# Scaling attention after P·V instead of scaling P, with heads sharing score banks, in a two-layer decoder kernel

## The chip, the cores and the metric

The kernel runs on one core of one Trainium2 chip. The metric is the device time of one execution in microseconds (us). Before the change it is 1733.85 us, the median of 3 runs (1732.92 to 1735.76). Engines are named as in the profile: PE is TensorE, DVE is VectorE, ACT is ScalarE, POOL is GpSimd, SP is SyncE.

## The reference

A decoder of two layers: width 1024, 512 tokens, float32. Each layer normalises x, projects it once, and feeds four token mixers of 4 heads x 64 whose outputs are joined and projected; then come cross attention over 256 memory rows and a SwiGLU.

```python
for l in range(DEPTH):
    h = rms_norm(x, norm_mix[l])
    c_hg, c_dsa, c_nsa, c_ml = split_cols(h @ w_in[l], GROUP_COLS)
    mixed = concatenate([hgrn2_mixer(c_hg, ...), dsa_mixer(c_dsa, ...), nsa_mixer(c_nsa, ...), mlstm_mixer(c_ml, ...)])
    x = x + mixed @ w_out[l]
    x = x + cross_attention(rms_norm(x, norm_xa[l]), rms_norm(mem, norm_mem[l]), ...)
    x = x + swiglu(rms_norm(x, norm_ffn[l]), ffn_w13[l], ffn_w2[l])

def masked_softmax(s, mask):
    s = where(mask, s, -inf);  m = max(s, -1);  e = exp(s - m)
    return e / sum(e, -1)

# DSA:  softmax(q k^T / 8, over the keys that an indexer picked) v
# NSA:  gate0 * softmax(q k_cmp^T / 8) v_cmp + gate1 * softmax(q k_sel^T / 8) v_sel + gate2 * softmax(q k_win^T / 8) v_win
# cross attention:  softmax(q k_mem^T / 8) v_mem
```

A softmax here is exp of the scores less their maximum, divided by its row sum; NSA multiplies each of its three outputs by a gate of each head and token. The HGRN2 mixer and the mLSTM mixer are recurrences in chunks and have no softmax over keys.

## The kernel before

**Tiling.** 512 tokens are 4 blocks of 128 (`tb` 0 to 3). Projections run as three products of split operands (xh·wh, xl·wh, xh·wl; lines L294 to L296 and L304 to L306). DSA and NSA attend blockwise: block `tb` sees the first `n = (tb + 1) * 128` keys. NSA calls `attend` twice in each block (selected keys, then window keys), DSA once: 12 calls in a layer. Cross attention (`xa`) has a loop of its own over the 4 blocks.

**One head in `attend`.** PE makes 128 x n scores in a PSUM bank `sc` (L513, L514) and adds the mask (L516 or L519). DVE takes the row maximum (L467). ACT makes P = exp(s - max) with the row sum (L469). DVE takes the reciprocal (L521) and multiplies P by it, in NSA by the gate too (L523, L525). PE transposes P in blocks of 128 x 128 into the bank `tp` (L458), ACT copies that to SBUF as PT (L462). After two heads PE multiplies with the values into the bank `o` (L533). The result is transposed: 64 rows for each head, 128 tokens along the free axis.

**Around it.** In DSA, `o` is split from PSUM into `xh` (ACT, L671) and `xl` (DVE, L672, recorded at the helper's line L316) for the output projection. In NSA a third, compressed attention (`compressed`, L1095 on) puts its output into the same bank `o` first (L1109); the two calls of `attend` accumulate onto it, and ACT copies the sum to `mo[2]` (L1124). `xa` handles two heads at a time: scores L1271 and L1272, maximum L1273, exp L1280, reciprocal L1282, scaling of P L1283 (at L316), transposes L458, P·V L1290, then xh L1298 and xl L1299 (at L316).

**PSUM.** In the stage with NSA the banks are `tp` 1, `sc` 2, `o` 1, `dt` 1, `mb` 1 and `acc` 2. In the stage with DSA they are `tp` 1, `sc` 1, `o` 1, `dt` 1, `hb` 2; there DSA's transposes go to `dt`. In `xa`: `tp` 2, `sc` 2, `o` 2.

**What sets the order.** Mixers are generators: their `yield` values are costs, and a weaver alternates between generators by these. The tile framework's scheduler then fixes one order of instructions for each engine. A layer has these stages (times of layer 0, then layer 1): the projection for DSA (0 to 30, then from 891.5); A, NSA and mLSTM with DSA's choice of keys (30 to 300.5; 892 to 1150.2), in which NSA attends from 117 and from 975; B, DSA's attention with HGRN2 and the first part of the output projection (300.5 to 430; 1150.2 to 1277); cross attention (430 to 500; 1277 to 1347); SwiGLU (500 to 891.5; 1347 to 1723). A last part of stage A (from 241 and from 1099.3, the "tail" below) has only NSA's block 3 and the end of mLSTM. L424 makes, in another stage, a factor for each token the same on all partitions: four float32 matmuls of a column against a diagonal.

Of the kernel before, what the change touches and what calls it, by code (L numbers as in the profile page):

```python
# [7 lines left out]
FT = mybir.dt.float32  # L8
# [3 lines left out]
AF = mybir.ActivationFunctionType  # L12
# [190 lines left out]
class Kernel:  # L203
# [260 lines left out]
    def softmax_unit(self, pool, sc, n, nmax, den):  # L464

        nc = self.nc
        nc.vector.tensor_reduce(nmax, sc[:, :n], axis=AX.X, op=OP.max, negate=True)  # L467
        p = self.t(pool, "P", [128, S], bufs=2)
        nc.scalar.activation(p[:, :n], sc[:, :n], AF.Exp, bias=nmax, accum_out=den)  # L469
        return p  # L470

# [30 lines left out]
    def attend(self, pool, tb, q, kst, v, mask, which, o, first, last, gate=None):  # L502

        nc = self.nc
        stat = self.t(pool, "stat", [128, 3, 4])
        n = (tb + 1) * 128
        for hp in range(2):
            pT = []  # L510
            for h in (2 * hp, 2 * hp + 1):
                sc = self.psum("sc", pool=pool)
                nc.tensor.matmul(sc[:, :n], q[0][:, h], kst[:, :n], start=True, stop=False, skip_group_check=True)  # L513
                nc.tensor.matmul(sc[:, :n], q[1][:, h], kst[:, :n], start=False, stop=False, skip_group_check=True)  # L514
                if mask is None:
                    nc.tensor.matmul(sc[:, n - 128:n], self.identb, self.trib, start=False, stop=True,  # L516
                                     skip_group_check=True)
                else:
                    nc.tensor.matmul(sc[:, :n], self.identb, mask, start=False, stop=True, skip_group_check=True)  # L519
                p = self.softmax_unit(pool, sc, n, stat[:, 0, h:h + 1], stat[:, 1, h:h + 1])  # L520
                nc.vector.reciprocal(stat[:, 2, h:h + 1], stat[:, 1, h:h + 1])  # L521
                if gate is None:
                    nc.vector.tensor_scalar(p[:, :n], p[:, :n], stat[:, 2, h:h + 1], None, op0=OP.mult)  # L523
                else:
                    nc.vector.tensor_scalar(p[:, :n], p[:, :n], stat[:, 2, h:h + 1], gate[:, h:h + 1],  # L525
                                            op0=OP.mult, op1=OP.mult)
                pT.append(self.t(pool, "PT", [128, S], bufs=3))
                ev = self.act_copy
                self.transpose_blocks(pT[-1][:, :n], lambda j: p[:, j * 128:j * 128 + 128], tb + 1, ev, pool=pool)
                yield 0.4 + 0.2 * tb  # L530
            for sb in range(tb + 1):
                for e in range(2):
                    nc.tensor.matmul(o[64 * e:64 * e + 64, hp], v(sb), pT[e][:, sb * 128:sb * 128 + 128],  # L533
                                     start=(first and sb == 0), stop=(last and sb == tb), skip_group_check=True)
            yield 0.2 + 0.2 * tb
# [89 lines left out]
    def dsa_attn(self, pool):  # L625
# [35 lines left out]
        for tb in range(TB):  # L661
            qb = nxt
            yield 1.0
            if tb < TB - 1:
                nxt = prepare(tb + 1)
            yield 1.0
            o = self.psum("o", (128, 2, 128))
            yield from self.attend(pool, tb, qb, kst, lambda sb: kv[:, sb, 64:128], masks[tb], 0, o, True, True)
            for c in range(2):
                (xh, xl), b = self.d_out[c], slice(tb * 128, tb * 128 + 128)  # L670
                nc.scalar.activation(xh[:, b], o[:, c], AF.Copy)  # L671
                self.tt(xl[:, b], o[:, c], xh[:, b].bitcast(FT), OP.subtract)  # L672
# [318 lines left out]
    def nsa(self, pool):  # L991
# [103 lines left out]
        def compressed(tb, e, o):  # L1095
# [11 lines left out]
            self.transpose_blocks(eT, lambda j: e.rearrange("p a b -> p (a b)"), 1, self.act_copy)  # L1107
            for hp in range(2):
                nc.tensor.matmul(o[:, hp], vbd[:, 2 * hp:2 * hp + 2].rearrange("p a b -> p (a b)"), eT,  # L1109
                                 start=(hp == 0), stop=False, skip_group_check=True)  # L1110

        nxt = prepare(0)
        for tb in range(TB):
            e, qb = nxt
            o = self.psum("o", (128, 2, 128))
            compressed(tb, e, o)
            yield 1.0
            for j, at in ((1, VS), (2, VW)):
# [3 lines left out]
                yield from self.attend(pool, tb, qb, kst[j - 1], lambda sb: tok[:, sb, at:at + 64], None, j,  # L1122
                                       o, False, j == 2, ga[:, tb, j])
            nc.scalar.activation(self.mo[2][:, :, tb * 128:tb * 128 + 128], o, AF.Copy)  # L1124
# [127 lines left out]
    def xa(self, pool, pw, rest):  # L1252
# [8 lines left out]
        for tb in range(TB):  # L1261
# [5 lines left out]
            for hp in range(2):  # L1267
# [14 lines left out]
                nc.vector.reciprocal(stat[:, 2, 2 * hp:2 * hp + 2], stat[:, 1, 2 * hp:2 * hp + 2])  # L1282
                self.tt(P, P, stat[:, 2, 2 * hp:2 * hp + 2, None].to_broadcast([128, 2, MEM]), OP.mult)  # L1283
# [186 lines left out]
```

## Time and profile before

| | |
|---|---|
| median of 3 runs | 1733.85 us |
| the profiled execution | 1724.88 us |
| its span | 1723.1 us |
| mean granted TensorE clock | 0.956 |
| PE busy | 1633.3 us (95%) |
| DVE busy | 989.5 us (57%) |
| ACT busy | 712.8 us (41%) |
| POOL busy | 793.5 us (46%) |

The profile is of one execution; what lies outside its span is 1.8 us. Busy time leaves out instructions that only wait or issue. Matmuls are pipelined: the step between the starts of two records tells more of their price than the duration of one.

### The profile page before, as it was taken

The numbers are of one execution on the slowest core, as the hardware profiler recorded it, in microseconds if no ns is written. First come the engines' busy times: TensorE is split into PE (matmuls) and PEld (weight loads), VectorE is DVE, ScalarE is ACT, GpSimd is POOL, SyncE is SP. The second block draws the span as 40 slices with busy tenths as digits, with TensorE's granted clock in tenths as the row PEclk, the third lists the DMA queues.
The fourth block names the chain that finished last, engine by engine and source line by source line (L and its number), as shares of the span: only waits on it lengthen the run. The fifth ranks groups of instructions, "written<-read, shape, count | busy, mean of one in ns | idle before, by whom it ended". The sixth has DMA issues, their size and how long they took to land.

```text
span 1723.1 us, 25048 instructions
## 1 busy us (share of the span) xinstructions
PE 1633.3 (95%) x9026; PEld 1347.7 (78%) x9030; DVE 989.5 (57%) x2022; ACT 712.8 (41%) x1545; POOL 793.5 (46%) x704
## 2 busy tenths in 40 slices
PE   7889989899899999999998899899998999999999
PEld 6778766687688888888897887677777888888887
DVE  5589974968774430343226999769768644114420
ACT  5445454326653322333444454542556433223321
POOL 5664441535715444444456644325364244444442
PEclk9999997959999999999999999898699999999999
DMA  5342211201503333333333422111032133332331
GB/s 158 99 116 87 68 57 38 66 13 32 163 13 98 96 91 95 98 93 92 98 108 98 114 79 62 57 50 46 28 97 64 50 93 94 93 100 92 97 103 64
DMA packets 83259, 140.38 MB, mean 81 GB/s; under 512 B 9528, under 2 KB 24632, under 8 KB 83136
## 3 DMA queue, kind: packets, MB, share of 16 engines
q1 hardware_dynamic: 80784, 133.81, 26.6%
q10 hardware_dynamic: 2032, 3.94, 0.7%
q8 instruction: 71, 1.16, 0.3%
q0 software_dynamic: 320, 1.05, 0.2%
q14 instruction: 52, 0.43, 0.1%
HBM read 134.55 MB, written 4.21 MB: 81 GB/s over the span
## 4 chain that ended last, share of the span: by engine, by line
PE 72%; DVE 14%; issue 6%; POOL 3%; DMA 3%; ACT 2%; SPq 0%; ACTq 0%; POOLq 0%; DVEq 0%
PE acc L295 11%; PE acc L296 11%; PE acc L294 11%; PE sc L295 5%; PE sc L296 5%; PE sc L294 5%; PE hb L770 3%; PE acc L304 3%; PE acc L306 3%; PE acc L305 3%; PE o L533 2%; DMA wr<-in_wst 2%; POOL wl L286 2%; PE tp L458 2%; PE mb L950 1%
## 5 line engine op out<-in xcount | busy, mean ns | idle before, releaser
L286 POOL TENSOR_TENSOR wl<-wr,wh 128x512 fp32r<-128x512 f32 (+5 forms) x504 | 633.4, 1265 | 627.2 <-ACT wh L285 589.4
L285 ACT ACTIVATE wh<-wr 128x512 fp32r<-128x512 f32 (+5 forms) x504 | 297.4, 597 | 508.0 <-PE acc L295 199.3
L294 PE MATMUL acc<-xh,wh 128*128 128x512 f32 (+1 forms) x704 | 271.3, 388 | 6.0 <-ACT wh L285 3.1
L295 PE MATMUL acc<-xl,wh 128*128 128x512 f32 (+1 forms) x704 | 272.2, 387 | 0.3 <-DVE xl L316 0.2
L296 PE MATMUL acc<-xh,wl 128*128 128x512 f32 (+1 forms) x704 | 271.7, 387 | 0.7 <-POOL wl L286 0.7
L431 DVE TENSOR_TENSOR xT<-acc,xT 128x512 f32<-128x512 f32 (+1 forms) x112 | 67.9, 611 | 214.3 <-PE acc L296 214.1
L294 PEld LDWEIGHTS acc<-xh,wh 128*128 128x128 f32 x704 | 131.9, 189 | 36.1 <-ACT wh L285 4.0
L295 PEld LDWEIGHTS acc<-xl,wh 128*128 128x128 f32 x704 | 132.5, 188 | 28.6 <-issue 1.0
L296 PEld LDWEIGHTS acc<-xh,wl 128*128 128x128 f32 x704 | 132.3, 188 | 28.3 <-POOL wl L286 1.6
L304 PE MATMUL acc<-wh,xh 128*128 128x256 f32 (+2 forms) x480 | 137.7, 289 | 4.1 <-DVE m_x L438 4.1
L295 PE MATMUL sc<-xl,wh 128*128 128x512 f32 x352 | 139.7, 397 | 0.0
L296 PE MATMUL sc<-xh,wl 128*128 128x512 f32 x352 | 138.8, 394 | 0.0
L296 PE MATMUL acc<-f_gh,wl 128*128 128x512 f32 x352 | 138.5, 395 | 0.0
L295 PE MATMUL acc<-f_gl,wh 128*128 128x512 f32 x352 | 138.4, 395 | 0.0
L294 PE MATMUL acc<-f_gh,wh 128*128 128x512 f32 x352 | 138.1, 394 | 0.0
L294 PE MATMUL sc<-xh,wh 128*128 128x512 f32 x352 | 138.0, 393 | 0.0
L305 PE MATMUL acc<-wl,xh 128*128 128x256 f32 (+2 forms) x480 | 137.6, 288 | 0.0
L306 PE MATMUL acc<-wh,xl 128*128 128x256 f32 (+2 forms) x480 | 137.1, 287 | 0.0
L1329 DVE SCALAR_TENSOR_TENSOR f_b<-sc,R 128x512 f32<-128x512 f32 x44 | 30.4, 691 | 127.5 <-PE sc L296 127.5
L304 PEld LDWEIGHTS acc<-wh,xh 128*128 128x128 f32 x480 | 90.9, 190 | 6.5 <-DVE m_x L438 4.5
L305 PEld LDWEIGHTS acc<-wl,xh 128*128 128x128 f32 x480 | 91.1, 190 | 0.7
L306 PEld LDWEIGHTS acc<-wh,xl 128*128 128x128 f32 x480 | 91.0, 190 | 0.7 <-issue 0.6
(395 smaller groups left out, 3183.3 us busy)
## 6 DMA issues: line engine op xcount, KB each, us to landing
wr<-in_wst SPq DMA_DIRECT2D x384, 256.0 KB, 2.6
wr<-in_wst SPq DMA_DIRECT2D x48, 128.0 KB, 2.6
wr<-in_wst SPq DMA_DIRECT2D x32, 192.0 KB, 2.4
wr<-in_wst SPq DMA_DIRECT2D x16, 262.0 KB, 2.7
wr<-in_wst SPq DMA_DIRECT2D x16, 148.0 KB, 2.2
wr<-in_wst SPq DMA_DIRECT2D x8, 264.0 KB, 2.8
m_Mb<-m_dram ACTq DMA_DIRECT2D x8, 256.0 KB, 3.3
memT<-in_memT SPq DMA_DIRECT2D x16, 128.0 KB, 2.1
```

The source lines that it names most:

```text
L285: nc.scalar.activation(hi, raw, AF.Copy)
L286: nc.gpsimd.tensor_tensor(lo, raw, hi.bitcast(FT), op=OP.subtract)
L294: self.nc.tensor.matmul(acc, wh, xh, start=(j == 0), stop=False)
L295: self.nc.tensor.matmul(acc, wh, xl, start=False, stop=False)
L296: self.nc.tensor.matmul(acc, wl, xh, start=False, stop=(j == n - 1))
L304: self.nc.tensor.matmul(acc, xh[:, s], wh, start=(first and j == 0), stop=False)
L305: self.nc.tensor.matmul(acc, xh[:, s], wl, start=False, stop=False)
L306: self.nc.tensor.matmul(acc, xl[:, s], wh, start=False, stop=(last and j == n - 1))
L431: self.nc.vector.tensor_add(self.xT[c][:, cols], acc, self.xT[c][:, cols])
L458: self.nc.tensor.transpose(p[:rows, j * 128:j * 128 + 128], src(j), self.ident)
L533: nc.tensor.matmul(o[64 * e:64 * e + 64, hp], v(sb), pT[e][:, sb * 128:sb * 128 + 128], start=(first and sb == 0), stop=(last and sb == tb ...
L770: nc.tensor.matmul(sc[s0:s1, b + t0:b + t1], kk[po:po + 64, b + s0:b + s1], qq[po:po + 64, b + t0:b + t1], start=True, stop=True)
```

## The change

`attend` no longer multiplies P by anything: exp(s - max) is transposed and multiplied with the values as it is. `G` heads (4, 2, 1, 1 in blocks 0 to 3) put their scores into one bank, one instruction of DVE takes their maxima, and their P share a tile, a set of transposes and a copy. After the four heads there is one reciprocal of 128 x 4, in NSA a multiplication by the gates. `spread` then makes, with four float32 matmuls of a factor column (broadcast to 64 columns) against the identity, a tile of 128 x 2 x 128 in `tp` that holds each head's and token's factor in the layout of `o`; ACT copies it to SBUF. DVE multiplies `o` by it. DSA and `xa` split that product into xh and xl; NSA adds it to `mo[2]`. NSA's compressed output goes to a `tp` bank of its own and is copied by ACT to `mo[2]`. One `o` bank now holds two outputs.

```diff
-                nc.vector.reciprocal(stat[:, 2, h:h + 1], stat[:, 1, h:h + 1])
-                if gate is None:
-                    nc.vector.tensor_scalar(p[:, :n], p[:, :n], stat[:, 2, h:h + 1], None, op0=OP.mult)
-                else:
-                    nc.vector.tensor_scalar(p[:, :n], p[:, :n], stat[:, 2, h:h + 1], gate[:, h:h + 1],
-                                            op0=OP.mult, op1=OP.mult)
...
+        G = (4, 2, 1, 1)[tb]
+        for h0 in range(0, 4, G):
+            sc = self.psum("sc", (128, G, n), pool=pool)
+            for e in range(G):
+                for j in range(2):
+                    nc.tensor.matmul(sc[:, e], q[j][:, h0 + e], kst[:, :n], start=(j == 0), stop=False,
+                                     skip_group_check=True)
...
+            nc.vector.tensor_reduce(stat[:, 0, h0:h0 + G], sc, axis=AX.X, op=OP.max, negate=True)
...
+            if h0 + G == 4:
+                nc.vector.reciprocal(stat[:, 2], stat[:, 1])
+                if gate is not None:
+                    self.tt(stat[:, 2], stat[:, 2], gate, OP.mult)
...
+        self.factor = self.spread(pool, stat[:, 2])
+
+    def spread(self, pool, f):
+        p = self.psum("tp", (128, 2, 128), pool=pool)
         for hp in range(2):
...
+            for e in range(2):
+                self.nc.tensor.matmul(p[64 * e:64 * e + 64, hp], f[:, 2 * hp + e:2 * hp + e + 1].to_broadcast([128, 64]),
+                                      self.ident, start=True, stop=True, skip_group_check=True)
+        out = self.t(pool, "spread", [128, 2, 128], bufs=1)
+        self.act_copy(out, p)
+        return out
+
+    def scaled_out(self, pool, tb, o, ks):
+        nc, b = self.nc, slice(tb * 128, tb * 128 + 128)
+        f = self.factor
+        self.tt(f, o, f, OP.mult)
+        for c, (xh, xl) in enumerate(ks):
+            nc.scalar.activation(xh[:, b], f[:, c], AF.Copy)
+            self.tt(xl[:, b], f[:, c], xh[:, b].bitcast(FT), OP.subtract)
...
+            o = self.psum("tp", (128, 2, 128))
             for hp in range(2):
                 nc.tensor.matmul(o[:, hp], vbd[:, 2 * hp:2 * hp + 2].rearrange("p a b -> p (a b)"), eT,
-                                 start=(hp == 0), stop=False, skip_group_check=True)
+                                 start=True, stop=True)
+            self.act_copy(self.mo[2][:, :, tb * 128:tb * 128 + 128], o)
...
-            nc.scalar.activation(self.mo[2][:, :, tb * 128:tb * 128 + 128], o, AF.Copy)
+                o = os[:, j - 1]
+                yield from self.attend(pool, tb, qb, kst[j - 1], lambda sb: tok[:, sb, at:at + 64], None, o, ga[:, tb, j])
+                f = self.factor
+                self.tt(f, o, f, OP.mult)
+                self.tt(out, out, f, OP.add)
...
-                nc.vector.reciprocal(stat[:, 2, 2 * hp:2 * hp + 2], stat[:, 1, 2 * hp:2 * hp + 2])
-                self.tt(P, P, stat[:, 2, 2 * hp:2 * hp + 2, None].to_broadcast([128, 2, MEM]), OP.mult)
...
+            nc.vector.reciprocal(stat[:, 2], stat[:, 1])
+            self.factor = self.spread(pool, stat[:, 2])
...
+            self.scaled_out(pool, tb, o, ks)
```

The change moves instructions at three places that the prediction speaks of. The first is PE at the start of NSA's block 3 in layer 0 (tp_2029, tp_2045: transposes of two heads' P; n_e: the compressed attention's weights). Before:

```order
L533 MATMUL o_1739<-PT_1921,n_tok_391 64x128
L533 MATMUL o_1739<-PT_1938,n_tok_391 64x128
L458 MATMUL tp_1965<-kc_314,n_e_1852 128x128
L513 MATMUL sc_2075<-n_kst0_795,qh_1867 128x512
L514 MATMUL sc_2075<-n_kst0_795,ql_1868 128x512
L516 LDWEIGHTS identb_316
L516 MATMUL sc_2075<-trib_318,identb_316 128x128
L965 MATMUL mb_3289<-m_v1_2181,m_p3_3261 128x65
L1109 MATMUL o_1953<-n_eT_1964,n_vbd_1251 128x128 x2
L458 MATMUL tp_2029<-kc_314,P_2024 128x128 x4
L458 MATMUL tp_2045<-kc_314,P_2040 128x128 x4
```

After:

```order
L533 MATMUL o_1713<-PT_1874,n_tok_391 64x128
L533 MATMUL o_1713<-PT_1889,n_tok_391 64x128
L543 MATMUL tp_1905<-kc_314,stat_1832 64x128 x4
L508 MATMUL sc_2032<-n_kst0_795,qh_1826 128x512
L508 MATMUL sc_2032<-n_kst0_795,ql_1827 128x512
L511 LDWEIGHTS identb_316
L511 MATMUL sc_2032<-trib_318,identb_316 128x128
L985 MATMUL mb_3257<-m_v1_2149,m_p3_3229 128x65
L458 MATMUL tp_1925<-kc_314,n_e_1811 128x128
L1130 MATMUL tp_1928<-n_eT_1924,n_vbd_1251 128x128 x2
L458 MATMUL tp_1990<-kc_314,P_1987 128x128 x4
```

Four uses of the one `tp` bank (spread, n_e, compressed output, P) now follow each other with five other rows between the first two and none after them; before, the compressed output went to `o`.

The second is PE at the boundary of stages A and B in layer 0 (acc_3650: the output projection's first product; mo3: mLSTM's output; xh_3489: the split of `mo[2]`). Before:

```order
L533 MATMUL o_1953<-PT_2165,n_tok_391 64x128
L1140 MATMUL tp_3525<-kc_314,mo3_106 128x128 x4
L634 MATMUL dt_3415<-one_321,ckvsq_3413 128x1 x4
L294 MATMUL acc_3650<-xh_3489,wh_3653 128x512
L294 MATMUL acc_3856<-xh_3489,wh_3859 128x512
```

After:

```order
L533 MATMUL o_1980<-PT_2123,n_tok_391 64x128
L543 MATMUL tp_2140<-kc_314,stat_2065 64x128 x4
L1165 MATMUL tp_3493<-kc_314,mo3_106 128x128 x4
L655 MATMUL dt_3383<-one_321,ckvsq_3381 128x1 x4
L294 MATMUL acc_3619<-xh_3457,wh_3622 128x512
L294 MATMUL acc_3787<-xh_3457,wh_3790 128x512
```

The last spread stands between the last P·V and the output projection, with no further row added to cover what follows it on ACT and DVE.

The third is DVE in the tail of layer 0, from one row maximum on (m_p: mLSTM's score products). Before:

```order
L958 SCALAR_TENSOR_TENSOR m_p1_3334<-mb_3327,m_d_3331 128x384
L525 TENSOR_SCALAR P_2105<-P_2105,stat_2099,n_ga_928 128x512
L467 TENSOR_REDUCE stat_2099<-sc_2140 128x1
L521 RECIPROCAL stat_2099<-stat_2099 128x1
L958 SCALAR_TENSOR_TENSOR m_p2_3343<-mb_3336,m_d_3340 128x256
L525 TENSOR_SCALAR P_2121<-P_2121,stat_2099,n_ga_928 128x512
L467 TENSOR_REDUCE stat_2099<-sc_2156 128x1
L958 SCALAR_TENSOR_TENSOR m_p3_3351<-mb_3345,m_d_3349 128x128
```

After:

```order
L525 RECIPROCAL stat_1981<-stat_1981 128x4
L316 TENSOR_TENSOR stat_1981<-stat_1981,n_ga_928 128x4
L978 SCALAR_TENSOR_TENSOR m_p1_3302<-mb_3295,m_d_3299 128x384
L513 TENSOR_REDUCE stat_2065<-sc_2080 128x1
L978 SCALAR_TENSOR_TENSOR m_p2_3311<-mb_3304,m_d_3308 128x256
L513 TENSOR_REDUCE stat_2065<-sc_2102 128x1
L978 SCALAR_TENSOR_TENSOR m_p3_3319<-mb_3313,m_d_3317 128x128
L316 TENSOR_TENSOR spread_2061<-o_1980,spread_2061 128x256
```

The multiplication of P no longer stands on DVE between a head's maximum and the next; the multiplication of the output does, once for four heads.

## Rows read from the trace of the kernel before

**Rows 1.** The page's busy line: share of the span and instructions of each engine.
```profile
PE 1633.3 (95%) x9026; PEld 1347.7 (78%) x9030; DVE 989.5 (57%) x2022; ACT 712.8 (41%) x1545; POOL 793.5 (46%) x704
```
**Rows 2.** Windows: from:to, length, busy PE, PEld, DVE, ACT, POOL, PEclk, DMA, GB/s.
```profile
117.00:300.50 183.50, 173.05 (x1125) 142.64 (x1124) 143.94 (x363) 90.97 (x229) 63.18 (x47) 0.92 0.20 60
...
975.00:1150.20 175.20, 166.15 (x1128) 136.28 (x1126) 144.38 (x366) 90.82 (x229) 63.75 (x47) 0.96 0.21 63
...
241.00:300.50 59.50, 49.41 (x281) 35.59 (x281) 36.95 (x89) 27.65 (x71) 13.27 (x12) 0.77 0.16 46
1099.30:1150.20 50.90, 44.35 (x289) 31.39 (x287) 35.36 (x89) 28.48 (x73) 12.80 (x11) 0.87 0.17 54
150.00:207.00 57.00, 56.65 (x326) 45.36 (x325) 56.52 (x127) 26.94 (x67) 28.30 (x18) 1.00 0.28 87
1000.00:1067.00 67.00, 64.50 (x386) 52.03 (x386) 66.72 (x144) 32.26 (x79) 33.98 (x23) 1.00 0.30 87
```
**Rows 3.** PE's waits: line, releaser, us in total, times, longest.
```profile
PE sc L1271 <- ACT P L1280: 9.1, 4, 3.4
...
PE o L533 <- ACT PT L462: 5.7, 6, 2.2
...
PE tp L458 <- ACT PT L462: 4.3, 6, 0.7
PE tp L458 <- DVE P L525: 3.5, 2, 2.8
```
**Rows 4.** Timeline of PE: start, us, engine, instruction [idle before, releaser]; eight-record groups.
```profile
1325.26 0.66 PE L1290 MATMUL o<-PT,x_v 128*64 128x128 f32 x8
1325.85 0.66 PE L458 MATMUL tp<-kc,P 128*128 128x128 f32 x4
...
523.42 1.05 PE L424 MATMUL tp<-kc,rcol 128*128 128x128 f32 x8
524.23 0.48 PE L295 MATMUL sc<-xl,wh 128*128 128x512 f32 x1
```
**Rows 5.** Timeline of PE around the start of a new group of matmuls.
```profile
1059.74 0.38 PE L304 MATMUL acc<-wh,xh 128*128 128x256 f32 x1
1059.96 0.28 PE L305 MATMUL acc<-wl,xh 128*128 128x256 f32 x1
1060.08 0.28 PE L306 MATMUL acc<-wh,xl 128*128 128x256 f32 x1
```
**Rows 6.** DVE by line: out<-in, shape, count | busy us, mean ns | idle before.
```profile
L525 DVE TENSOR_SCALAR P<-P,stat,n_ga 128x128 f32<-128x128 f32 (+3 forms) x64 | 35.5, 554 | 1.3
...
L523 DVE TENSOR_SCALAR P<-P,stat 128x128 f32<-128x128 f32 (+3 forms) x32 | 15.8, 494 | 0.4
L521 DVE RECIPROCAL stat<-stat 128x1 f32<-128x1 f32 x96 | 14.8, 154 | 14.9 <-ACT P L469 14.8
L316 DVE TENSOR_TENSOR P<-P,x_stat 128x512 f32<-128x512 f32 x16 | 11.0, 688 | 0.2
...
L316 DVE TENSOR_TENSOR mo<-mb,m_den 128x256 f32<-128x256 f32 x8 | 3.4, 423 | 0.2
```
**Rows 7.** Timeline of DVE and PE in the tail of layer 0.
```profile
249.70 1.42 DVE L525 TENSOR_SCALAR P<-P,stat,n_ga 128x384 f32<-128x384 f32 x1
...
251.26 0.87 PE L458 MATMUL tp<-kc,P 128*128 128x128 f32 x3 [2.75 <-DVE P L525]
...
281.99 0.66 PE L458 MATMUL tp<-kc,P 128*128 128x128 f32 x4 [0.75 <-ACT PT L462]
```
**Rows 8.** Timeline at the boundary of stages A and B, layer 0: ACT, then PE.
```profile
300.56 0.38 ACT L1124 ACTIVATE mo<-o 128x256 f32<-128x256 f32 x1 [1.18 <-PE o L533]
...
302.43 0.71 PE L294 MATMUL acc<-xh,wh 128*128 128x512 f32 x2
```
**Rows 9.** Timeline at the end of cross attention, layer 1: PE, ACT.
```profile
1341.15 0.66 PE L1290 MATMUL o<-PT,x_v 128*64 128x128 f32 x8
...
1341.85 0.28 ACT L1298 ACTIVATE xh<-o 128x128 fp32r<-128x128 f32 x1 [1.40 <-PE o L1290]
```

More of the change, by code (lines that the diff above doesn't have):

```diff
@@ L462, in act_copy @@
         self.nc.scalar.activation(out, in_, AF.Copy)
[L464 to L470, printed above, removed]
     def k_stack(self, pool, k, name):
@@ L500, in q_split, with attend @@
         return qh, ql
-    def attend(self, pool, tb, q, kst, v, mask, which, o, first, last, gate=None):
+    def attend(self, pool, tb, q, kst, v, mask, o, gate=None):
         nc = self.nc
@@ L508, in attend @@
         n = (tb + 1) * 128
-        for hp in range(2):
[L510 to L517, printed above, removed]
-                else:
-                    nc.tensor.matmul(sc[:, :n], self.identb, mask, start=False, stop=True, skip_group_check=True)
-                p = self.softmax_unit(pool, sc, n, stat[:, 0, h:h + 1], stat[:, 1, h:h + 1])
-                nc.vector.reciprocal(stat[:, 2, h:h + 1], stat[:, 1, h:h + 1])
-                if gate is None:
-                    nc.vector.tensor_scalar(p[:, :n], p[:, :n], stat[:, 2, h:h + 1], None, op0=OP.mult)
-                else:
-                    nc.vector.tensor_scalar(p[:, :n], p[:, :n], stat[:, 2, h:h + 1], gate[:, h:h + 1],
-                                            op0=OP.mult, op1=OP.mult)
[L527 to L535, printed above, removed]
@@ new lines, in attend @@
+        G = (4, 2, 1, 1)[tb]
+        pT = {}
+        for h0 in range(0, 4, G):
[4 more added lines that the diff above has]
+                                     skip_group_check=True)
+                m = self.trib if mask is None else mask
+                nc.tensor.matmul(sc[:, e, n - m.shape[1]:], self.identb, m, start=False, stop=True,
+                                 skip_group_check=True)
+            nc.vector.tensor_reduce(stat[:, 0, h0:h0 + G], sc, axis=AX.X, op=OP.max, negate=True)
+            p = self.t(pool, "P", [128, S], bufs=2)
+            for e in range(G):
+                h = h0 + e
+                nc.scalar.activation(p[:, e * n:e * n + n], sc[:, e], AF.Exp, bias=stat[:, 0, h:h + 1],
+                                     accum_out=stat[:, 1, h:h + 1])
+            pt = self.t(pool, "PT", [128, S], bufs=3)
+            self.transpose_blocks(pt[:, :G * n], lambda j: p[:, j * 128:j * 128 + 128], G * (tb + 1), self.act_copy,
+                                  pool=pool)
+            for e in range(G):
+                pT[h0 + e] = pt[:, e * n:e * n + n]
+            if h0 + G == 4:
+                nc.vector.reciprocal(stat[:, 2], stat[:, 1])
+                if gate is not None:
+                    self.tt(stat[:, 2], stat[:, 2], gate, OP.mult)
+            yield G * (0.4 + 0.2 * tb)
+            if (h0 + G) % 2 == 0:
+                for hp in range((h0 + G - 1) // 2 if G < 4 else 0, (h0 + G) // 2):
+                    for sb in range(tb + 1):
+                        for e in range(2):
+                            nc.tensor.matmul(o[64 * e:64 * e + 64, hp], v(sb), pT[2 * hp + e][:, sb * 128:sb * 128 + 128],
+                                             start=(sb == 0), stop=(sb == tb), skip_group_check=True)
+                    yield 0.2 + 0.2 * tb
@@ new lines, in attend @@
+        self.factor = self.spread(pool, stat[:, 2])
+    def spread(self, pool, f):
+        p = self.psum("tp", (128, 2, 128), pool=pool)
+        for hp in range(2):
+            for e in range(2):
+                self.nc.tensor.matmul(p[64 * e:64 * e + 64, hp], f[:, 2 * hp + e:2 * hp + e + 1].to_broadcast([128, 64]),
[3 more added lines that the diff above has]
+        return out
@@ L666, in dsa_attn @@
             yield 1.0
[L667 to L672, printed above, removed]
+            if tb % 2 == 0:
+                os = self.psum("o", (128, 2, 2, 128))
+            o = os[:, tb % 2]
+            yield from self.attend(pool, tb, qb, kst, lambda sb: kv[:, sb, 64:128], masks[tb], o)
+            self.scaled_out(pool, tb, o, self.d_out)
         self.attn_done = True
@@ L1093, in prepare, with compressed @@
             return e, self.q_block(pool, q)
-        def compressed(tb, e, o):
+        def compressed(tb, e):
             cs = self.t(pool, "n_cs", [128, 3, 4])
@@ L1114, in nsa @@
             e, qb = nxt
-            o = self.psum("o", (128, 2, 128))
-            compressed(tb, e, o)
+            compressed(tb, e)
             yield 1.0
+            out = self.mo[2][:, :, tb * 128:tb * 128 + 128]
+            os = self.psum("o", (128, 2, 2, 128))
             for j, at in ((1, VS), (2, VW)):
@@ L1294, in xa @@
                 ks = [tuple(self.xs.tile([128, S], FR, name=n, tag="x") for n in ("xh", "xl")) for c in range(2)]
-            b = slice(tb * 128, tb * 128 + 128)
-            for c in range(2):
-                xh, xl = ks[c]
-                nc.scalar.activation(xh[:, b], o[:, c], AF.Copy)
-                self.tt(xl[:, b], o[:, c], xh[:, b].bitcast(FT), OP.subtract)
+            self.scaled_out(pool, tb, o, ks)
             yield 3.0
```

2 lines of the change are left out of this document (removed).

## The prediction

> **What bounds the kernel now.** I read the busy line first. PE works 1633.3 us of a span of 1723.1, so all its idle time in the whole kernel is 89.8 us, while DVE works 989.5 [rows 1]. The reader is to see that two prices count on different scales: a microsecond of PE work is added to the time almost in full, and a microsecond taken from DVE counts only where PE was waiting for it.
>
> Next came the windows. In the two stretches in which NSA attends, PE is busy 173.05 of 183.50 us and 166.15 of 175.20 [rows 2], so about 10.4 and 9.0 us are idle there. Two stretches within them need a look of their own: in 150 to 207 and in 1000 to 1067 DVE is busy 56.52 of 57.00 us and 66.72 of 67.00, with PE at 56.65 and 64.50 [rows 2]. There both engines are full, and one cannot say from the windows alone which paces the other. The third thing in the windows is the clock. The tail of layer 0 takes 59.50 us with a mean granted clock of 0.77; the same work in layer 1 takes 50.90 us at 0.87 [rows 2]. The clock is in those means a mix of its two levels, 2.4 and 1.2 GHz, and PE had idled before it fell: in the tail of layer 0 PE waited 2.75 us for DVE's P just ahead of 251.26 [rows 7].
>
> Then PE's waits, summed over the whole span. Those that the change can touch are scores of cross attention waiting for exp to free a bank, 9.1 us; P·V waiting for PT, 5.7; transposes waiting for the PT copy to free `tp`, 4.3; transposes waiting for P to be scaled in NSA, 3.5 [rows 3]. Together 22.6 us. That is the measure of what can be won by waits. The removed scaling itself is behind only 3.5 of it.
>
> **The change part by part.** Sums are made on the profiled execution, 1724.88 us (1.8 us of it outside its span). The median of the three runs, 1733.85, is 8.97 above that; I add the sum of the change to the median.
>
> *Removed from DVE.* L525 35.5 us (64 x 554 ns), L523 15.8, 96 reciprocals 14.8, the scaling of cross attention's P 11.0 [rows 6]: 77 us. *Added to DVE*: 32 multiplications of 128 x 256 with one operand in PSUM, by the like of mo<-mb,m_den 423 ns each, 13.5 us; 16 additions of 128 x 256 for NSA, by the same row 7; 28 small ones of about 154 ns or a bit more, 5 [rows 6]. Net about -51 us on DVE. At its own engine I cost that at nothing, since PE is the engine that ends last; what it wins is in the waits and in the clock, below. The cover for it is PE's own work.
>
> *Added to PE: spread.* 4 DSA, 8 NSA and 4 cross-attention spreads in each of 2 layers are 32, each four float32 matmuls that stand as eight records. The trace has no spread. Eight records of the same shape, alternating halves of the array likewise, are P·V of cross attention: from its start at 1325.26 to the next instruction at 1325.85 are 0.59 us [rows 4]. L424, a column against a diagonal with 128 columns, takes 0.81 us from 523.42 to 524.23 [rows 4]. I take 0.59, as the shape is the same: 32 x 0.59 = +18.9 us. Bounds: 0 (if every one fell into time in which PE stood idle anyway; a gain is excluded, work is only added) and 32 x 0.81 = 25.9 at full clock.
>
> *Merged heads.* Per attend of blocks 0 and 1, groups of four and of two heads save starts: five groups of scores less (3 in block 0, 2 in block 1) and five of transposes; six attends of each block in two layers (2 NSA and 1 DSA each) make 60 starts fewer. At the start of a group the step is longer than within it: 0.22 us from 1059.74 to 1059.96, against 0.12 from there to 1060.08 [rows 5]. So a start costs 0.1 more: -6 us; bounds 0 (the number of matmuls is the same, and a start can hide behind an idle time) and -12 (if the step into the group is longer as well). A gathered group also means that the maximum comes only after all four heads' scores; other generators' rows stand in between, and I cost it at nothing; uncovered, it would be one wait of about 0.75, the price of a turn [rows 7], in each of 12 attends, 9 us.
>
> *Waits that go.* All of the 3.5 us for scaled P; of the 10.0 us for PT, about half, as P reaches the transposes earlier by a scaling of 0.55 us; of the 9.1 us for exp in cross attention a quarter [rows 3], as the bank is freed by exp, which the change leaves where it is, and only DVE is less busy before it. 3.5 + 5.0 + 2.3 = -10.8 us. Bounds 0 (what is late next is the copy of PT on ACT, which stays and now shares ACT with 32 spread copies) and -22.6.
>
> *The clock in the tails.* In the tail of layer 0 the last L525s meet a busy DVE: one takes 1.42 us, and PE waits behind it [rows 7]. Without it the tail of layer 0 could run as that of layer 1: 59.5 - 50.9 = 8.6 us [rows 2]. The third order listing shows the multiplication gone from between one maximum and the next. But P·V's other waits for ACT remain, so I take a third, -3. Bounds -12 (both tails gain) and +8.6 (layer 1's tail falls to layer 0's clock).
>
> *New chains, three of them.* (a) At the end of cross attention the last xh now comes after a spread, its copy and a multiplication. Before, it came 0.70 us after the start of the last P·V, at 1341.85 [rows 9]; the extra steps are a copy like L1124's 0.38 [rows 8] and a multiplication of 0.42, and PE's cover there also becomes shorter, six rows of projection instead of twelve. About +1 per layer, +2; bounds 0 and +4. (b) At the start of NSA's block 3, spread, n_e, the compressed output and P go through the single `tp` bank one after another, with no row of other work between the last three (first order listing). A turn of that bank shows as an idle time of 0.75 us at 281.99 [rows 7]. Two turns more in each layer: +3. Bounds 0 and 32 x 0.75 = +24, if every spread meets its neighbours in that bank. (c) At the boundary of A and B the output projection's first product needs `mo[2]` of the last block. Before, ACT's copy of 0.38 us at 300.56 leads to the product at 302.43 [rows 8]. Now the spread (0.59, counted above), its copy (0.38), a multiplication (0.42) and an addition (0.42) stand in place of that one copy, and no row was added on PE to cover them (second listing): 0.84 more, with two more handovers between engines some 1.5 per layer, +3; bounds 0 and +4.
>
> **A rule that speaks against this change.** The row: PE idled 0.75 us at 281.99 until the copy of PT had emptied `tp` [rows 7]. The Trainium skill, "Perfetto Trace Analysis", section "Optimizing Tensor Performance / Matmuls", states that independent matmul groups should rotate through different PSUM banks so that the evacuation of one overlaps the next group's matmuls. The trace agrees at that row. By that rule the sum would carry the 24 us of (b) in place of its 3; it is the fourth case below.
>
> **The sum.** 18.9 - 6 - 10.8 - 3 + 2 + 3 + 3 = +7.1 us: 1732.0 for an execution like the profiled one, 1741 on the scale of the median.
>
> **The rivals.**
>
> *Faster: waits and clock.* If all 22.6 us of waits go, the tail of layer 0 gets its 8.6 us and the rest stays (18.9 - 6 + 8 of the new chains), the sum is -10.3; with the starts at 0.2 and half the new chains it is about -20. Taken between: -14, so 1720. For it: PE's idle before a low clock is the kind of wait that the change removes, and DVE loses 51 us of work. Against it: only 3.5 us of all waits name the scaled P, and 19.1 of the 22.6 name an ACT operation that stays.
>
> *DVE paces the two full stretches.* In 150 to 207 and 1000 to 1067 DVE never rests. If it, not PE, sets their length, they shrink by the work taken out inside them. They are 124 of the 358.7 us in which NSA attends [rows 2], about a third. NSA's 64 heads lose 35.5 us of scaling and 9.9 of reciprocals, its 16 attends gain some 18: a third of -27 is -9, and 7.1 - 9 gives about -2, 1732. Against it: PE is busy 56.65 of 57.00 us in the first at full clock [rows 2], so PE itself leaves no room there; only the second has 2.5 us.
>
> *The bank serialises (slower).* Mechanism: spread, transposes and compressed output share one `tp` bank in stages A and B, and each spread holds it until ACT has copied; PE, in order, waits. Price 0.75 us for each of 32; it decides from about a third of them on (8 us more). 7.1 - 3 + 24 = +28: 1762. For it: tp is already waited for 4.3 us [rows 3]. Against it: elsewhere rows of mLSTM or HGRN2 stand between, as the five between spread and n_e in the listing.
>
> *Layer 1's tail falls to layer 0's clock (slower).* New idle at block 3's start lets the clock fall earlier in layer 1, and neither tail gains: +7.1 + 3 + 8.6 is about +19, 1753. For it: in layer 0 the same work at the lower clock took 8.6 us more, after idle times of 2.75 and 0.75 us [rows 7]. Against it: each has less DVE work than before.
>
> **How the numbers follow.** Two runs of this kernel differ by up to 0.16%, so under 0.2% (3.5 us) nothing can be told. Chances: forecast 0.42 (1741, its own range 1735 to 1748), waits and clock 0.24 (1720), DVE-paced 0.12 (1732), bank 0.10 (1762), clock in layer 1 0.12 (1753). Faster than 1730.4: 0.24 + 0.04 of the third case + 0.02 of the forecast's lower end = 0.30. Between 1730.4 and 1737.3: 0.07 of the third, 0.12 of the forecast = 0.19. Slower: 0.51. The range runs from 1719, which leaves out the lower part of the second case, to 1758, which leaves out most of the fourth: under 0.2 together.
>
> **What would show it.** PE's busy time up by 12 to 19 us with 32 groups of L543 of about 0.6 us each: the price of spread is right. DVE's down by about 50 us without a gain like it: DVE was not the pace. No wait on PE for a scaled P. Waits of PE at L1130, L543 or L458 for a `tp` bank: chain (b), and if they sum to over 8 us, the fourth case. The tail from 241 on shorter by more than 6 us at a clock over 0.85: the second case. L294 at the boundary and at the end of cross attention later by about 1 us each after the last P·V. I am wrong if PE's busy time stays or falls, or if the stretches full on DVE shrink by more than a few microseconds.

## The result and the profile after

The changed kernel takes 1703.82 us (median of 4 runs, 1700.13 to 1713.08) against 1733.38 before (4 runs, 1732.20 to 1735.76): a ratio of 0.985, interval 0.980 to 0.989. I had forecast 1741. The change is 1.5% faster where I expected 0.4% slower. The profiled execution is of 1700.13 us, span 1698.4, against 1724.88 and 1723.1. (Medians and means below leave out the few executions that were disturbed.)

The busy line, as [rows 1]:

```profile
PE 1614.4 (95%) x9281; PEld 1340.0 (79%) x9286; DVE 950.0 (56%) x1864; ACT 723.1 (43%) x1547; POOL 792.5 (47%) x704
```

TensorE runs 255 records more and is busy 18.9 us less. Work was added and the busy time fell, so the next view is span and granted clock, before and then after:

```profile
core 0: 1723.1 us, clock 0.956
```

```profile
core 0: 1698.4 us, clock 0.969
```

The two levels are 2.4 and 1.2 GHz, and at the lower one a matmul takes about twice as long. If TensorE sets the pace, span x clock is the time that the same work would take at the full level, and the rest is what the low level cost. Before: 1723.1 x 0.956 = 1647 and a loss of 76. After: 1698.4 x 0.969 = 1646 and a loss of 53. The work is as long as before, and 23 of the 24.7 us are clock. (An estimate, as it takes TensorE for the pace; in DSA's low stretches it was busy nearly all the time, below.)

Where did the clock come back? I compare the same stretches in both kernels: NSA's two as in [rows 2], then the one from DSA's first score to its last P·V. What the weaver puts beside the attention in them is not quite the same work. Columns are those of [rows 2]. Of the kernel before, the DSA stretch of layers 0 and 1 and the part of each in which the low level was granted:

```profile
332.30:423.50 91.20, 86.66 (x596) 71.52 (x598) 70.25 (x169) 38.14 (x110) 39.05 (x47) 0.79 0.09 25
1182.60:1273.50 90.90, 84.69 (x565) 68.26 (x567) 69.05 (x166) 39.87 (x114) 42.21 (x46) 0.79 0.09 27
342.00:379.60 37.60, 36.99 (x148) 30.36 (x147) 24.01 (x61) 6.76 (x24) 9.61 (x13) 0.50 0.01 4
1195.40:1232.90 37.50, 37.50 (x218) 29.98 (x217) 25.28 (x62) 11.26 (x37) 15.29 (x21) 0.50 0.04 11
```

Of the changed kernel, NSA's stretches of both layers, the DSA stretches, and the low part of the first of these:

```profile
113.70:290.00 176.30, 167.43 (x1195) 140.69 (x1196) 133.30 (x327) 93.10 (x227) 62.71 (x53) 0.94 0.21 64
959.50:1140.10 180.60, 167.40 (x1188) 140.56 (x1188) 136.30 (x323) 93.93 (x227) 63.78 (x53) 0.93 0.20 61
327.70:408.20 80.50, 76.50 (x586) 64.43 (x589) 58.46 (x125) 40.26 (x111) 41.05 (x45) 0.83 0.10 29
1172.80:1243.30 70.50, 69.64 (x592) 57.41 (x595) 58.35 (x128) 39.80 (x110) 40.73 (x46) 1.00 0.14 42
...
333.60:360.90 27.30, 24.59 (x107) 20.63 (x108) 17.08 (x42) 9.33 (x30) 7.90 (x10) 0.50 0.04 14
```

The DSA stretch took 91 us in each layer at a mean clock of 0.79, 37.5 us of it at 1.2 GHz with TensorE busy throughout. After, it takes 80.5 us with 27 low, and 70.5 us with none: -31 us, more than the whole gain. Clock is 24 us of that: low time fell from 75.1 to 27.3 us, and half of low time is loss. The other 7 us are work that went or moved to other stretches, which the windows do not tell apart. NSA's stretches went from 183.50 to 176.30 at 0.94 in place of 0.92, and from 175.20 to 180.60 at 0.93 in place of 0.96: layer 0 got some clock back, layer 1 lost some, and in clock they nearly cancel. In layer 1 the low level of the tail begins about 1.5 us after a wait of a kind that the change brought in, for the copy of a spread to free `tp`:

```profile
1093.16 0.44 PE L458 MATMUL tp<-kc,n_tok 128*128 128x128 f32 x2 [2.70 <-ACT spread L462]
```

```profile
1094.50:1111.60 17.10, 11.57 (x42) 7.28 (x42) 11.17 (x23) 7.76 (x21) 4.68 (x3) 0.51 0.00 1
```

Cross attention, from first score to last P·V, went from 27.70 and 27.60 us to 30.10 and 30.90.

What TensorE did before the clock fell is on its timeline. Before, in DSA's block 0, layer 0 and then two turns of layer 1:

```profile
341.85 0.30 PE L458 MATMUL dt<-kc,P 128*128 128x128 f32 x1 [2.28 <-DVE ql L316]
...
1193.35 0.30 PE L458 MATMUL dt<-kc,P 128*128 128x128 f32 x1 [0.98 <-DVE ql L316]
1194.61 0.33 PE L513 MATMUL sc<-kst,qh 128*128 128x128 f32 x1 [0.96 <-ACT P L469]
...
1195.05 2.18 PE L770 MATMUL hb<-h_qs,h_ks 64*128 64x128 f32 x13
```

The first two waits are of the transposes, for VectorE's split of the next block's q to empty the bank `dt`; the third is for exp to free the only `sc` bank. In layer 0 the low level begins at 342.0, right after the wait of 2.28 us. In layer 1 it begins 0.8 us after the start of the scores that had waited. After, in layer 0, there is one wait left in block 0, and the low level begins inside it:

```profile
330.73 1.71 PE L790 MATMUL hb<-h_qs,h_ks 64*128 64x128 f32 x16
336.31 0.82 PE L458 MATMUL dt<-kc,P 128*128 128x128 f32 x2 [3.87 <-ACT P L517]
```

In layer 1 after, no wait for DSA's P or for `sc` is recorded at all between 1140 and 1243.3. TensorE's waits in the kernel after that answer to [rows 3]:

```profile
PE tp L458 <- ACT P L1305: 7.5, 4, 2.8
...
PE o L533 <- ACT PT L462: 4.7, 6, 2.5
...
PE tp L458 <- ACT PT L462: 2.3, 4, 0.7
```

The wait for the scaled P is gone. Cross attention's wait moved from the scores (9.1 us) to the transposes (7.5 us): the bank is no longer waited for, exp is.

The price of spread, as [rows 4], at the full level and in the low stretch of layer 0:

```profile
1187.05 0.61 PE L543 MATMUL dt<-kc,stat 128*64 128x128 f32 x8
1187.58 0.51 PE L294 MATMUL acc<-xh,wh 128*128 128x512 f32 x1
...
343.93 1.07 PE L543 MATMUL dt<-kc,stat 128*64 128x128 f32 x8
344.93 0.58 PE L790 MATMUL hb<-h_qs,h_ks 64*128 64x128 f32 x1
```

0.53 us at 2.4 GHz and 1.00 at 1.2 GHz, against 0.59 foreseen. What DVE was given in place of [rows 6]:

```profile
L316 DVE TENSOR_TENSOR spread<-o,spread 128x256 f32<-128x256 f32 x32 | 13.5, 421 | 19.4 <-ACT spread L462 18.5 <-PE o L1313 0.5
...
L316 DVE TENSOR_TENSOR mo<-mo,spread 128x256 f32<-128x256 f32 x16 | 7.9, 493 | 0.1
```

At the boundary of stages A and B, as [rows 8]:

```profile
289.76 0.70 PE L543 MATMUL tp<-kc,stat 128*64 128x128 f32 x7
...
292.52 0.74 PE L294 MATMUL acc<-xh,wh 128*128 128x512 f32 x2
```

From the start of the last group of P·V to that product it was 299.44 to 302.43, 2.99 us; now it is 288.94 to 292.52, 3.58 us. The 0.59 more is about the spread itself; the chain of copy, multiplication and addition hid behind mLSTM's transposes. In layer 1 it did not hide whole: the same distance went from 3.00 us (1149.18 to 1152.18) to 4.07 (1139.09 to 1143.16), with a wait for the split of `mo`:

```profile
1143.16 0.73 PE L294 MATMUL acc<-xh,wh 128*128 128x512 f32 x2 [0.50 <-ACT xh L1160]
```

### The profile page after: what moved, and what is told of

It reads as the page before. It is cut to its first block, busy times and chain, and to the rows that moved or that the text cites. A ratio compares the mean times of both kernels' runs of the same rounds, so it can differ in the third digit from the quotient of the medians.

```text
span 1698.4 us, 25369 instructions
## 1 busy us (share of the span) xinstructions
PE 1614.4 (95%) x9281; PEld 1340.0 (79%) x9286; DVE 950.0 (56%) x1864; ACT 723.1 (43%) x1547; POOL 792.5 (47%) x704
```

## The experiments

Theory M: the gain is the low clock that left DSA's stretch, and what removed it are the merged heads: four turns through the one score bank become one in block 0 and two in block 1. Rival S: it is the scaling of P taken off VectorE. Theory C, beneath M: TensorE's idle turns drop the clock, and the clock is the price. All runs were timed beside the kernel before.

The table gives the median, the ratio with its interval (to the executions of the kernel before that were timed beside the run), and the means of span x clock ("full") and of the rest ("loss") over the executions. The last column is the mean clock of the DSA stretch in layers 0 and 1; it is of one execution of each kernel, the profiled one.

| kernel | us | ratio | full | loss | DSA clock |
|---|---|---|---|---|---|
| before (38 executions) | 1728.3 | 1 | 1642.5 | 84.3 | 0.79, 0.79 |
| changed | 1703.8 | 0.985 (0.980 to 0.989) | 1648.5 | 55.0 | 0.83, 1.00 |
| e1, nothing merged | 1751.3 | 1.012 (1.009 to 1.014) | 1663.3 | 85.4 | 0.77, 1.00 |
| e2, merging alone | 1700.7 | 0.983 (0.980 to 0.987) | 1637.5 | 61.5 | 0.84, 0.86 |
| e3, DSA not merged | 1745.7 | 1.009 (1.007 to 1.011) | 1645.2 | 98.2 | 0.77, 0.78 |
| e4, slower P | 1712.4 | 0.990 (0.988 to 0.993) | 1644.2 | 66.3 | 0.85, 0.89 |
| e5, late scaling in DSA alone | 1695.0 | 0.980 (0.977 to 0.983) | 1639.4 | 52.2 | 1.00, 1.00 |
| e6, two score banks, not merged | 1710.9 | 0.990 (0.987 to 0.993) | 1646.6 | 62.7 | 0.76, 1.00 |
| e7, DSA merged in block 0 alone | 1737.2 | 1.005 (1.002 to 1.008) | 1651.9 | 83.1 | 0.73, 0.92 |
| e8, cross attention as before | 1706.1 | 0.988 (0.985 to 0.992) | 1638.1 | 68.0 | 0.85, 0.93 |
| e9, before + useless matmuls | 1706.2 | 0.988 (0.984 to 0.991) | 1655.7 | 48.6 | 1.00, 0.92 |
| e10, changed + useless matmuls | 1710.4 | 0.989 (0.984 to 0.993) | 1654.1 | 52.2 | 0.98, 1.00 |
| e11, e5 + two score banks | 1688.6 | 0.978 (0.975 to 0.981) | 1642.2 | 45.3 | 1.00, 1.00 |

Read down "full" and "loss": "full" lies within 18 us of one another in all but e1, while "loss" runs from 45 to 98. In the last column the three kernels whose DSA heads all take single turns through one bank (before, e1, e3) have five of six stretches at 0.77 to 0.79, those merged in both blocks without further edit to DSA (changed, e2, e5, e8) have all eight at 0.83 or above. Which stretch of a kernel goes low is not explained by it: e1 has one at 1.00.

**e1: heads not merged, late scaling kept.**

```diff
-        G = (4, 2, 1, 1)[tb]
+        G = 1
```

> The changed kernel with G = 1 in every block: scores, maximum and transposes head by head again, the scaling after P.V kept. Theory M (the gain came from the merged heads: in DSA's block 0 four round trips through the one score bank became one, and TensorE no longer idles there and no longer falls to its low clock): the stretch from DSA's first score to its last P.V is about 91 us again in both layers with some 37 us at the low clock, and the time is about 1725 to 1735. Theory S (the gain came from taking the scaling of P off VectorE): at most 6 us slower than the changed kernel (60 group starts of 0.1 us), about 1706 to 1712, with the DSA stretch still at 70 to 80 us.

It is slower than the kernel before, at the same loss. So the late scaling without the merging costs 1663.3 - 1642.5 = 20.8 us at full clock and gives nothing back. Theory S is wrong. Theory M is not right in its detail: the time is 16 us above its range, and the DSA stretch is long and low in layer 0 only (95.90 us at 0.77; 73.50 us at 1.00 in layer 1), while NSA's stretches lost more than before.

**e2: merging alone.** The kernel before with the changed kernel's loop over groups, and in it the old scaling. Shown against the changed kernel:

```diff
+            for e in range(G):
+                h = h0 + e
+                pe = p[:, e * n:e * n + n]
+                nc.vector.reciprocal(stat[:, 2, h:h + 1], stat[:, 1, h:h + 1])
+                if gate is None:
+                    nc.vector.tensor_scalar(pe, pe, stat[:, 2, h:h + 1], None, op0=OP.mult)
...
-        self.factor = self.spread(pool, stat[:, 2])
```

> The kernel before with merged heads alone: P is still scaled on VectorE, head by head, before its transposes; no spread, nothing on the outputs; cross attention as before. Theory M: the DSA stretch falls to 70 to 80 us and the time is 1690 to 1708, below the changed kernel, since the 32 spreads (12 to 19 us of TensorE) are not there. Theory S: about 1727 to 1733, the starts' 6 us at most.

As theory M had it, the whole gain is there: -5.0 us at full clock and -22.8 of loss. VectorE scales every P there, as before. With the merging in place, the late scaling costs 11.0 us at full clock (1648.5 - 1637.5) and gives back 6.5 of loss.

**e3: merged in NSA, not in DSA.**

```diff
-        G = (4, 2, 1, 1)[tb]
+        G = (4, 2, 1, 1)[tb] if gate is not None else 1
```

> The changed kernel with G = 1 in DSA alone, NSA merged. Theory M with the place named (DSA): as the first kernel of this set, some 15 to 25 us slower than the changed kernel, all of it in the DSA stretches. If the merging matters in NSA instead: within 4 us of the changed kernel. Theory S: within 4 us.

42 us slower than the changed kernel, at about its full-clock time. Its DSA stretches are back where they were before the change:

```profile
337.60:427.00 89.40, 84.69 (x589) 70.56 (x589) 61.64 (x135) 40.86 (x116) 42.40 (x47) 0.77 0.09 25
1195.40:1289.80 94.40, 90.00 (x606) 72.69 (x607) 64.22 (x139) 42.26 (x119) 43.08 (x47) 0.78 0.10 30
```

The 15 to 25 us foreseen were too few: the loss rose in NSA's tails as well.

**e7: DSA merged in block 0, not in block 1.**

```diff
-        G = (4, 2, 1, 1)[tb]
+        G = (4, 2, 1, 1)[tb] if gate is not None else (4, 1, 1, 1)[tb]
```

> The changed kernel with DSA merged in block 0 alone (four heads), block 1 head by head. Theory: block 0 is where the kernel before idled and dropped its clock, so 1703 to 1715, near the changed kernel. Rival: block 1's pairs matter as much, 1718 to 1735 (halfway to the 1746 of DSA unmerged) or more.

The rival holds: with block 0 alone merged the loss is 15 us below e3's, and merging the pairs of block 1 too brings the other 28 of the 43 us down to the changed kernel. In the profiled execution block 0 alone helped in layer 1 only (0.92; layer 0 has 0.73).

**e6: the kernel before with two score banks in DSA.** Heads are not merged; the odd ones use `tp`, which DSA does not use in that stage.

```diff
-                sc = self.psum("sc", pool=pool)
+                sc = self.psum("tp" if gate is None and h % 2 else "sc")
```

> The kernel before, with DSA's score matmuls alternating between the bank sc and the bank tp (which that stage leaves idle), heads not merged, P scaled as before. Theory B (what the merging mends is the four serial turns through one score bank in DSA's block 0 and 1; a second bank mends half of it): the DSA stretch falls from 91 to about 75 to 85 us and the time to 1705 to 1722. Rival G (it is the number of groups and generator steps, or the order the scheduler makes of larger units, not the bank): within 5 us of the kernel before.

The time is in theory B's range, and rival G's is out: loss 62.7 against 84.3, 21.6 us less, nearly the 22.8 us of merging alone, by another bank alone. So the turns through the one bank are at least part of what the merging mends. That they are all of it is not shown: in the profiled execution only layer 1's stretch is at full clock, layer 0's stays at 0.76, and in the kernel before the recorded waits for exp to free `sc` in the two DSA stretches sum to 1.2 us, all in layer 1. This is the rule on rotating banks seen from the other side: the Trainium skill, "Perfetto Trace Analysis", section "Optimizing Tensor Performance / Matmuls", asks for another bank so that evacuation and matmuls overlap, and that worked here; sharing a bank between several heads worked as well (e2).

**e9: the kernel before with work added.** Nothing reads the result.

```diff
+                if gate is None and tb < 2:
+                    d = self.psum("tp")
+                    for j in range(4):
+                        nc.tensor.matmul(d[:, j * 128:j * 128 + 128], stat[:, 0, h:h + 1].to_broadcast([128, 128]),
+                                         self.ident, start=True, stop=True, skip_group_check=True)
```

> The kernel before with work that nothing reads added to TensorE: in DSA's blocks 0 and 1, after each head's maximum, four float32 matmuls of 128x128 (some 0.81 us, the price of L424's group) into the idle tp bank; 16 groups in two layers, +13 us of TensorE work. Theory C (the low clock in DSA's stretch, 37.5 us in each layer, is what the time was lost to, and it follows from TensorE's idle turns): the added work fills the turns, the low clock shrinks in those stretches, and the kernel is not 13 us slower but within 5 us of before or faster, 1710 to 1733. Rival W (the turns themselves, not the clock, cost the time; added work is added time): 1738 to 1745.

This run speaks most directly for theory C, and against rival W. TensorE does 13.2 us more work at full clock, as priced (16 x 0.81), and the kernel is 22 us faster, because 36 us of loss are gone. The added groups stand where the turns were; one of them, and TensorE's windows over the two DSA stretches:

```profile
340.39 1.16 PE L524 MATMUL tp<-kc,stat 128*128 128x128 f32 x8
341.31 0.31 PE L513 MATMUL sc<-kst,qh 128*128 128x128 f32 x1
```

```profile
334.40:416.50 82.10, 78.85 (x667) 66.11 (x666) 70.88 (x167) 40.35 (x112) 40.81 (x47) 1.00 0.10 31
1177.00:1260.30 83.30, 80.51 (x632) 67.32 (x631) 69.12 (x165) 38.82 (x113) 42.62 (x46) 0.92 0.09 27
```

The clock is 1.00 and 0.92 where it was 0.79, and the stretches are 8 to 9 us shorter with 6.6 us more work in each. (The edit also gives the scheduler other rows to order; what that alone does was not tested.) That idle turns between groups of matmuls make the clock swing is what the Trainium skill, "TensorE: Matmul & The Clock Gate", section "A second HAM failure mode: psum-queue depth-cycling", tells of another kernel; the trace agrees.

**e10: the changed kernel with such work** (after each maximum of DSA's blocks 0 and 1).

```diff
+            if gate is None and tb < 2:
+                d = self.psum("tp")
+                for e in range(8):
+                    nc.tensor.matmul(d[:, e % 4 * 128:e % 4 * 128 + 128], stat[:, 0, h0:h0 + 1].to_broadcast([128, 128]),
+                                     self.ident, start=True, stop=True, skip_group_check=True)
```

> The changed kernel with eight such matmuls (1.6 us) after each maximum of DSA's blocks 0 and 1, ahead of the transposes that waited 3.87 us for P in layer 0; 6 groups in two layers, +10 us of work. Theory C: layer 0's low stretch of 27 us goes, 13 us back for 10 us paid: 1695 to 1706. Rival W: 1710 to 1715.

The time is the rival's: 5.6 us of work more, 2.8 of loss less. Theory C's forecast for layer 0 held in the one profiled execution, of 1726.01 us: its DSA stretch is at 0.98 in place of 0.83. But with 13 us of loss to win there the mean loss fell by 2.8 only; where the rest stood in the other executions is not shown. Where the turns are already few, filler did not pay.

**e4: the changed kernel with a slower P** in one block of layer 1:

```diff
+            if self.l == 1 and gate is None and tb == 0:
+                for _ in range(6):
+                    nc.scalar.activation(p, p, AF.Copy)
```

> The changed kernel with six extra in-place ScalarE copies of P (128x512, some 0.6 us each, 3.6 us in all) in DSA's block 0 of layer 1 alone, the stretch that ran at full clock throughout. Theory C (an idle TensorE there drops the clock, and the low clock is the price, not the wait): low clock of 20 to 40 us appears in layer 1's DSA stretch and the time rises by 10 to 20 us. Rival: only the wait itself counts, or other work covers it: 0 to +4 us and no low clock there.

+8.6 us, just under theory C's 10 to 20, and 11 of loss. In the profiled execution, of 1729.41 us, layer 1's DSA stretch is at 0.89 in place of 1.00. But the run decides nothing: the scheduler put other rows into the gap that it foresaw, so TensorE's order changed too.

**e8: cross attention as before**, the rest changed.

```diff
+                nc.vector.reciprocal(stat[:, 2, 2 * hp:2 * hp + 2], stat[:, 1, 2 * hp:2 * hp + 2])
+                self.tt(P, P, stat[:, 2, 2 * hp:2 * hp + 2, None].to_broadcast([128, 2, MEM]), OP.mult)
...
-            self.factor = self.spread(pool, stat[:, 2])
```

> The changed kernel with cross attention as before (P scaled, no spread there). Cross attention took 2.4 and 3.3 us more in the two layers after the change (8 spreads of 0.59 us are 4.7 of these 5.7), the clock there was the same: 5 to 6 us faster than the changed kernel, 1696 to 1700. Rival: the scheduler's order elsewhere shifts and the clock hides it, within 3 us of the changed kernel or slower.

No gain in time, against 5 to 6 us foreseen: 10.4 us less at full clock, of which cross attention's two stretches explain 5.7, and 13 of loss more; in the profiled execution it shows in stretches that the edit doesn't touch (DSA's in layer 1 has 0.93 in place of 1.00). The rival holds.

**e5 and e11: a better version.** NSA as in e2, DSA as in the changed kernel, cross attention as before (e5, against e2); in e11 DSA's score groups alternate between `sc` and `tp` too.

```diff
-            for e in range(G):
+            for e in range(G if gate is not None else 0):
...
+        if gate is None:
+            self.factor = self.spread(pool, stat[:, 2])
...
+            self.scaled_out(pool, tb, o, self.d_out)
```

```diff
-            sc = self.psum("sc", (128, G, n), pool=pool)
+            sc = self.psum("tp" if gate is None and h0 // G % 2 else "sc", (128, G, n))
```

> Heads merged everywhere; NSA scales P before its transposes as the kernel before (compressed output accumulated in the same bank), DSA scales its output by spread as the changed kernel, cross attention as before. Sum from the runs so far: at full clock the merging alone was worth -5.5 us and the late scaling +11 (32 spreads); here 8 of 32 spreads remain, so some 1640 us at full clock, and the loss to the low clock 45 to 60 us: 1685 to 1700, the fastest so far. Rival (late scaling in NSA is what saves the clock): 1700 or more.

> The mixed kernel (heads merged everywhere, late scaling in DSA alone) with DSA's score groups alternating between the banks sc and tp as well. Theory: what is left of serial turns is blocks 1 to 3 of DSA, where the mixed kernel's trace shows no low clock any more, so little is left: 1690 to 1697, within 5 us of the mixed kernel. Rival: the second bank is worth its own 17 us again, under 1685.

e5 came out in its range, e11 a little below its own. e11 is the fastest: 1688.6 us, 2.2% below the kernel before. Its DSA stretches run at full clock and are the shortest of all:

```profile
327.80:388.10 60.30, 60.30 (x542) 49.82 (x541) 50.47 (x112) 34.53 (x97) 32.09 (x38) 1.00 0.09 25
1161.70:1227.30 65.60, 64.61 (x553) 52.48 (x554) 56.60 (x125) 37.14 (x102) 36.19 (x40) 1.00 0.11 31
```

## Why the prediction was wrong, step by step

- **Bound and scale.** TensorE's work counts in full, VectorE's only where TensorE waits. This held: 39.5 us left VectorE (about 51 foreseen), and e1 shows no gain from it. My own sign of being wrong came true all the same: TensorE's busy time fell, by 18.9 us. I had read busy time as work; the clock is in it.
- **Spread, +18.9.** Right for one spread: 0.53 us each is 17.0 us. The whole late scaling, with what it saves, is 20.8 us at full clock without merging (e1) and 11.0 with it (e2).
- **Merged heads, -6.** About right at full clock: -5.0 in e2, though the starts were not measured by themselves. But in the same paragraph I cost the changed shape of the turns, one wait in place of four, at nothing and bounded it only as a loss of 9 us. It is what gave the gain: 22.8 us of loss in e2.
- **Waits, -10.8.** The scaled P's 3.5 us went, PT's 10.0 became 7.0, and cross attention's 9.1 became 7.5 at another place: 8.1 us. New waits ate part of it: 3.87 us for DSA's P in layer 0, the wait of a gathered group that I had cost at nothing, and those of (b) below. All of TensorE's idle time went only from 89.8 to 84.0 us.
- **Clock, -3 with bounds -12 and +8.6: the step that failed.** I worked it out for the two tails of stage A alone. There it was small, as forecast, with layer 0 gaining and layer 1 losing. The DSA stretches, low for 37.5 us in each layer before, stood in no term and in no rival. They became 10.7 and 20.4 us shorter, 24 us of it by the clock, against 23 us of clock in the whole kernel. In [rows 2] I had shown only NSA's stretches.
- **New chains, +8.** (a) In layer 1, from the start of the last P·V to SwiGLU's first product into `sc`, it is 5.52 us (1316.04 to 1321.56) in place of 5.16 (1341.15 to 1346.31), with six rows of projection fewer in between, about 0.7 us at 0.12 each: some 1 us, as foreseen, though I had misread one row: the xh at 1341.85 is the first of the last block's two, and the last starts at 1342.49. Ahead of it cross attention became 5.7 us longer, of which 8 spreads are 4.2; the other 1.5 was in no term. (b) New waits for the `tp` bank are 2.7 us for a spread's copy and 0.9 for `mo`'s: 3.6 for 3. (c) The boundary cost nothing beyond the spread in layer 0 and 0.5 in layer 1, for 3. Together "full" of the changed kernel is 6.0 above before, where my sum without the clock term was +10.1.
- **Rivals.** "Waits and clock" had the direction and a wrong place. "DVE paces" is out by e1. "The bank serialises" was real at a few places, 3.6 us and not 24; a bank that serialises mattered more in the kernel before, where a second one for DSA's scores took 21.6 us of loss off (e6). "Layer 1's tail" came in part: NSA's stretch there became 5.4 us longer, with the new wait of 2.70 us ahead of the low level.

Open: why a layer's stretch goes low in one kernel and not in another (e6 and e1 keep 0.76 and 0.77 in layer 0 and have 1.00 in layer 1), which of the waits ahead of a low stretch matters (for `dt` or for `sc`), and why merging NSA alone (e3) loses more than merging nothing (e1).

## What to carry to other kernels

Before an edit is priced, list every stretch at the low clock level, with what TensorE did ahead of it, and ask of each whether the edit touches that; a stretch can be busy throughout and run at half the clock. Split each time into span x clock and the rest: here added or saved work showed in the first and the shape of the turns mostly in the second, and the second was nearly five times as large. Where several heads take turns through one PSUM bank, try fewer, larger groups or a second bank before taking work off an engine that is not the bound: here these gave back 22.8 and 21.6 us of loss, and 39.5 us off VectorE gave none.

## What the runs showed that I had not expected

Added work made the kernel faster: 16 groups of matmuls that nobody reads, 13 us, took 22 us off (e9). And the time of one kernel varies with its clock: the changed one between 1700.13 us (0.969) and 1713.08 us (0.964), with full-clock times of 1646 to 1652. The 38 executions of the kernel before run from 1722.18 to 1736.05 us, 0.8% and not the 0.16% that I had taken for the noise.
